# A two-layer decoder trunk on one core: longer planner estimates, all low parts on VectorE, other warming products

## The chip, the cores and the metric

The kernel runs on one core of one Trainium2 chip. The metric is the device time of one execution in microseconds (us), smaller being better. A core has a matrix engine (TensorE, PE in the rows; PEld is its weight load), VectorE (DVE), ScalarE (ACT), GpSimd (POOL) and SyncE (SP), which here issues the weight DMAs. Each engine works through its own instructions in the order in which the program holds them and waits on semaphores for the others.

## What is computed

256 tokens of width 1024 go through two layers in float32. Cut to what matters:

```python
for layer in range(2):
    y = h @ w_in[layer]                       # 3672 columns, split among three head groups
    out_a = gla_mixer(...)                    # gated linear attention, 4 heads, chunks of 64
    out_b = moba_mixer(...)                   # one causal block of 256: softmax attention, 4 heads
    out_c = dsa_mixer(...)                    # indexer scores, the best 64 keys of a query, softmax
    mix = concat(out_a, out_b, out_c) @ w_out[layer]
    h = layer_norm(2 ** 0.5 * h + mix)
    h = layer_norm(2 ** 0.5 * h + moe_ffn(h)) # 16 experts, best group, top 2, SiLU gate, d_ff 512
```

The DSA group keeps, for each query, the keys whose indexer score is among the 64 highest, and takes a softmax over them alone.

## The kernel before

**Stages.** A layer has a mixer stage (projections, the three mixers, the product with `w_out`) and an expert stage. The two token tiles of 128 rows are t = 0 and 1. All weights stream in over SP into 33 buffers of 512 KB and some small ones; a buffer's next load is issued when its last reader is done.

**Projections.** A weight slice of 128 x 512 is split into a high part (`whi`, ScalarE) and a low part (`wlo`, the difference) by `Pieces.fill`, four slices ahead of their use (three for `w_out`). Three products per token tile (high by high, high by low, low by high) make one projection (`pj`, `gq`, `gk`; `po` with `w_out`). The keys come in the order I (indexer), V, GV, M (MoBA's q and k), S (DSA's q and k), GK, GG. Low parts are made by VectorE, save each fifth from the 25th slice on, which GpSimd makes (`SHARE`, `FROM`, line 593): 13 a layer, and two more at the start of layer 1.

**Order.** The instructions of the mixer stage are not written in one order. `backbone` runs the projections, and tasks run beside it: `indexer` (scores, then eight rounds of MAX and MATCH_REPLACE on `acc` a tile, t = 1 first), `qk`, `decays`, `linear`, `gated`, and `attend`, which calls `softmax_pv` for S and M. Class `Order` keeps a clock per engine, advanced by `_Lane.cost`, an estimate in ns for each instruction. A task goes on as soon as what it waits for is due by PE's estimated clock. The rounds of the selection have one more condition, line 877: the estimated clock of VectorE may be at most 400 ns ahead of PE's. `attend` for S starts when the selections of both tiles are made (`done.add("sel")`).

**Softmax.** `softmax_pv` does t = 0 and then t = 1, each in full: four score products (`sc<-qkT`), on VectorE four row maxima with the mask (`s_sb,mx<-sc`), on ScalarE four exponentials, on VectorE the reciprocals and four scalings, on PE the transposes (`pT`), on ScalarE their copies; and at the end the products with the values (`pv`) and the split of the result into `mx` high and low.

**Output product.** `OUT_ORDER` is (4, 6, 2, 0): the two blocks of MoBA, then those of S, which wait for the split of S, then those of GLA (`mxG`).

**Routing.** After `po`, `close_mix` adds the residual, turns the result (`tr`), forms the router's logits (`lgT`, `lg`), and `score` applies a Sigmoid (`sc<-lg`). A one-element Sigmoid at the end of `gated` (tile `warm`) has ScalarE load that function's table ahead of time. `choose` picks experts and `xT` gathers tokens.

**Warming.** `warm(n, w)` issues 2n products of 128 x 128 whose result nobody reads: 14 at the start, 4 ahead of the routing's result in each layer, 8 between the layers.

Of the kernel before, what the change touches and what calls it, by code (L numbers as in the profile page):

```python
# [9 lines left out]
F32 = mybir.dt.float32  # L10
# [34 lines left out]
N_T4 = 9  # L45
N_SM = 10
N_WS = 4
SHARE = 5
FROM = 24
N_WO = 3  # L50
N_UNITS = ((1, 3), (2, 6))
N_WARM0 = 7
N_AHEAD = 5
LAG = 350.0
TRIG = 5487.999999999999
N_FILL = 2
N_LAST = 2
N_WARM = 2
N_LEAD = 7
N_WARM2 = 4  # L60
TWO = (1, 3, 5)
AGAIN = {(0, 'g', 5), (1, 'g', 2), (1, 'g', 0), (1, 'd', 1), (1, 'd', 6), (1, 'd', 4), (2, 'g', 3), (2, 'd', 6)}
FILL = (1, 2)
# [13 lines left out]
class Order:  # L77
# [24 lines left out]
    def note(self, lane, cost, ins, outs):  # L102
        start = self.clk[lane]
        for a in ins:
            t, who = self.ready.get(a.tensor.name, (0.0, lane))
            start = max(start, t + (self.NEAR[lane] if who == lane else self.FAR))
        end = start + cost
        self.clk[lane] = end
        for a in ins + outs:
            n = a.tensor.name  # L110
            if n in self.held:
                self.held[n] = max(self.held[n], end)
        for a in outs:
            self.ready[a.tensor.name] = max((end, lane), self.ready.get(a.tensor.name, (0.0, lane)))
# [74 lines left out]
class _Lane:  # L189
# [3 lines left out]
    def cost(self, name, out, ins, kw, scalars=0):  # L193
        def free(a):
            n = 1
            for s in a.shape[1:]:
                n *= s
            return n
        n = free(out)
        psum = any(i.space == bass.MemoryType.PSUM for i in ins)  # L200
        if self.lane == "PE":
            if name == "transpose":
                return 110.0
            f = 1.68 if ins[0].dtype == F32 else 0.42
            c = max(214.0 if ins[0].dtype == F32 else 100.0, f * n)
            if out.shape[0] <= 64 and ins[0].shape[0] <= 64 and n <= 128:
                return max(50.0, f * n / 2)
            return c / 2 + 20 if out.shape[0] <= 64 and ins[0].shape[0] > 64 else c
        if self.lane == "ACT":
            return 0.833 * n + (52 if psum else 94) + 93 * (scalars + ("accum_out" in kw))  # L210
        if self.lane == "POOL":
            if name == "memset":
                return 0.8 * n + 70
            return 165.0 * n + 300 if kw.get("op") == OP.pow else 2.2 * n + 50
        m = max([n] + [free(a) for a in ins])
        if name == "reciprocal":
            return 6.3 * n + 68
        if name in ("tensor_scalar", "tensor_copy") and not psum:
            return 0.54 * n + 65 + 61 * scalars
        return 1.04 * m + 65 + 61 * scalars  # L220

    def __getattr__(self, name):
        fn = getattr(self.e, name)
# [20 lines left out]
def trunk_kernel(ctx, tc, x, positions, w_in, gate_up, gate_bias, norm_gain, w_out, ln_mix_g, ln_mix_b,  # L244
# [8 lines left out]
    pe, act, dve, pool = od.pe, od.act, od.dve, od.pool  # L253
# [4 lines left out]
    def bank(name="ps"):  # L258
        b = pp.tile([P, 512], F32, name=name, tag="ps")
        od.take(b.tensor.name)  # L260
        return b

    def t2(name, shape=(P, 512), dt=F32):
        return wp.tile(list(shape), dt, name=name, tag="t2", bufs=N_T2)
# [80 lines left out]
    def more(n=1):  # L345
        for _ in range(n):
            while issued[0] < len(specs) and specs[issued[0]][0] in extra:
                issued[0] += 1
            if issued[0] >= len(specs):
                return  # L350
            key, (parts, nk, w) = specs[issued[0]]
            issued[0] += 1
            t = fp.tile([P, nk, w], F32, name="wf", tag="wf")
            for at, src in parts:
                nc.sync.dma_start(t[:, at[0], at[1]] if at else t.rearrange("p k n -> p (k n)"), src)
            feed[key] = t
# [66 lines left out]
    ident = cp.tile([P, P], F32, name="ident")  # L423
# [77 lines left out]
    def mm(o, a, b, start=True, stop=True):  # L501
        pe.matmul(o, a, b, start=start, stop=stop, skip_group_check=True)
# [59 lines left out]
    def warm(n, w):  # L562

        b_ = bank("warm")
        for i in range(2 * n):
            mm(b_[:, 0:P], w, ones)
        od.free(b_)

# [8 lines left out]
    class Pieces:  # L577
# [8 lines left out]
        def fill(self, eng=dve):  # L586
            while self.i < len(self.plan) and self.i < self.j + self.ahead:
                key, kk, c0, n = self.plan[self.i]
                src = feed[key][:, kk, c0:c0 + n]
                hi = t2("whi", (P, n), F32R)  # L590
                lo = t2("wlo", (P, n), F32R)
                act.activation(hi, src, AF.Copy)
                (pool if self.i % SHARE == SHARE - 1 and self.i >= FROM else eng).tensor_sub(lo, src, hi.bitcast(F32))
                units[key] = feed[key]
                self.made[self.i] = hi, lo
                self.left[key] -= 1
                if not self.left[key]:
                    feed.pop(key)
                    more()
                self.i += 1  # L600
# [72 lines left out]
    def weight_pieces(l):  # L673
        plan = []
        for key in ORDER:
            _, groups, cols = CHUNKS[key]
            for i, nk in enumerate(groups):
                plan += [((l, key, i), kk, cols[0] * j, n) for kk in range(nk) for j, n in enumerate(cols)]
        for k0 in OUT_ORDER:
            plan += [((l, "O", k0 + kk), 0, 512 * n, 512) for kk in range(2) for n in range(2)]  # L680
        return Pieces(plan, N_WS)
# [75 lines left out]

    units, begun = {}, set()
    warm(N_WARM0, ones)
    pieces = weight_pieces(0)  # L760
    hhi, hlo = halves(0)
# [4 lines left out]
    for l in range(DEPTH):  # L766
# [529 lines left out]
        def choose(t):  # L1296

            s, g = slice(t * E, t * E + E), slice(4 * t, 4 * t + 4)
            top1, top2 = (top[:, i:i + 1] for i in (2 * t, 2 * t + 1))
            x4 = sel[:, s].rearrange("p (g e) -> p g e", e=4)  # L1300
            xa, xj = (x4[:, :, :, None].to_broadcast([P, 4, 4, 4]), x4[:, :, None, :].to_broadcast([P, 4, 4, 4]))
            rank4 = rank[:, s].rearrange("p (g e) -> p g e", e=4)
            yield dve.tensor_add(sel[:, s], sc[:, s], rb)
            dve.tensor_add(sums[:, g, 0:2], x4[:, :, 0:2], x4[:, :, 2:4])
            dve.tensor_add(sums[:, g, 2:4], x4[:, :, 0::2], x4[:, :, 1::2])
            rev = bass.AP(tensor=sel.tensor, offset=sel.offset + t * E + 3, ap=[sel.ap[0], [4, 4], [-1, 2]])
            yield dve.tensor_add(sums[:, g, 4:6], x4[:, :, 0:2], rev)
            dve.tensor_reduce(gs[:, g], sums[:, g], AX.X, OP.max)
            yield dve.tensor_tensor(gt[:, g], xj, xa, op=OP.is_gt)
            dve.tensor_reduce(top1, gs[:, g], AX.X, OP.max)  # L1310
            yield dve.tensor_tensor(ge[:, g], xj, xa, op=OP.is_ge)
            dve.scalar_tensor_tensor(at[:, g], gs[:, g], top1, pref[:, 0:4], op0=OP.is_equal, op1=OP.mult)
            yield dve.copy_predicated(gt[:, g], below[:, None].to_broadcast([P, 4, 4, 4]), ge[:, g])
            dve.tensor_reduce(top2, at[:, g], AX.X, OP.max)
            yield dve.tensor_reduce(rank4, gt[:, g], AX.X, OP.add)
            yield dve.tensor_scalar(at[:, g], at[:, g], top2, None, op0=OP.is_ge)
            yield dve.scalar_tensor_tensor(hot[:, s].rearrange("p (g e) -> p g e", e=4), rank4, 1.5,
                                           at[:, g, None].to_broadcast([P, 4, 4]), op0=OP.is_lt, op1=OP.mult)
            if t == 0:
                mm(pc[:, 0:E], strict, hot[:, 0:E])  # L1320
            else:
                mm(pc[:, E:2 * E], strict, hot[:, E:2 * E])
            yield dve.tensor_scalar(pos[:, s], hot[:, s], -1000.0, 1000.0, op0=OP.mult, op1=OP.add)
            yield dve.tensor_add(pos[:, s], pos[:, s], pc[:, s])
# [165 lines left out]
        dve.tensor_scalar(mvs[1][:, 4:5], mvs[1][:, 0:1], mvs[1][:, 3:4], -1.0, op0=OP.mult, op1=OP.mult)  # L1490
        act.activation(h[1], h[1], AF.Identity, scale=mvs[1][:, 3:4], bias=mvs[1][:, 4:5])
        warm(N_WARM, ident)
        for _ in steps[0]:
            next(steps[1])
# [68 lines left out]
        for p in range(E // 2):  # L1563
# [54 lines left out]
            for i in range(8):  # L1618
                n, k = (i // 4, i % 4) if p >= FIN - 1 else (i % 2, i // 2)
# [39 lines left out]
        if last:  # L1659
            finish(z, sb, sts, *vecs[2:])  # L1660
            break
        warm(N_WARM2, ident)

        def close(t, z, st, hhi, hlo, nxt=l + 1, sb=sb, g2=vecs[2], b2=vecs[3]):
# [56 lines left out]
```

## Time and profile before

| what | value |
|---|---|
| median of 3 runs | 717.87 us (717.22 to 718.00) |
| profiled execution | 717.56 us, of which the span from the first to the last instruction 715.5 us |
| PE busy in the span | 687.1 us (96%) |
| VectorE, ScalarE, GpSimd busy | 443.9 us, 273.6 us, 75.0 us |
| mean granted TensorE clock | 0.993 of full speed |
| mixer stages, read off the timeline | about 6.8 to 148 us and 357 to 500 us |

A matmul's end in the trace is modelled, so PE busy time can hold short waits; the idle time before an instruction, in square brackets with what ended it, is what PE visibly waited. Float32 products show as two instructions each. Times in a timeline row are the start in the span and the length.

### The profile page before, as it was taken

What the parts mean: (1) busy time and instruction counts of PE and PEld (TensorE: products, weight loads), DVE (VectorE), ACT (ScalarE), POOL (GpSimd) and SP (SyncE); (2) the same over time, 40 slices, a digit from 0 to 9 for tenths busy, and PEclk for the clock granted to TensorE, in tenths of its full rate; (3) what the DMA queues carried; (4) which work ended last, traced back from release to release, by engine and by line L of the source; (5) the groups of instructions that cost most, each with busy time, mean ns of one, the idle gap of its engine ahead of it and who ended that gap; (6) DMA issues with size and microseconds to landing.
All of it is one profiled execution on the core that took longest, in us unless ns stands there. A gap on an engine that the chain in (4) does not pass through costs nothing. (4 is left out here: it accounts for less than half of the span.)

```text
span 715.5 us, 11300 instructions
## 1 busy us (share of the span) xinstructions
PE 687.1 (96%) x3885; PEld 399.2 (56%) x3885; DVE 443.9 (62%) x1091; ACT 273.6 (38%) x579; POOL 75.0 (10%) x102
## 2 busy tenths in 40 slices
PE   9999999999999989999899999999999999899993
PEld 8887878843533533533487879787435334343330
DVE  6778887652445454767487787867243556259646
ACT  5578675431212201212276676564223022022121
POOL 2021022200000001200121111121000000021002
PEclk9999999999999999999999999999999999999997
DMA  9799937979999999999999844479899999999971
GB/s 306 272 388 407 408 120 250 325 293 408 409 403 408 407 407 408 408 410 407 334 391 401 313 154 146 132 251 338 323 408 408 403 407 409 407 407 409 409 288 59
DMA packets 83533, 244.05 MB, mean 341 GB/s; under 512 B 10180, under 2 KB 14344, under 8 KB 83464
## 3 DMA queue, kind: packets, MB, share of 16 engines
q1 hardware_dynamic: 82792, 242.91, 89.0%
q8 instruction: 34, 0.56, 0.3%
q10 hardware_dynamic: 416, 0.26, 0.1%
q14 instruction: 35, 0.29, 0.1%
q0 software_dynamic: 256, 0.03, 0.0%
HBM read 242.13 MB, written 1.05 MB: 340 GB/s over the span
## 5 line engine op out<-in xcount | busy, mean ns | idle before, releaser
L239 PE MATMUL gu<-wf,xT 128*64 128x512 f32 x912 | 226.0, 594 | 3.6 <-PEq L1437 3.6
L239 DVE SCALAR_TENSOR_TENSOR yt<-y,ws,yt 32x512 fp32r<-32x512 f32 (+1 forms) x116 | 86.7, 748 | 94.9 <-ACT yt L239 93.4
L239 PEld LDWEIGHTS gu<-wf,xT 128*64 128x64 f32 x912 | 71.8, 137 | 131.7 <-issue 123.3
L239 DVE TENSOR_TENSOR wlo<-wf,whi 128x512 fp32r<-128x512 f32 (+3 forms) x148 | 89.6, 640 | 39.5 <-ACT whi L239 28.5
L239 PE MATMUL y<-wf,actT 128*64 128x512 f32 x432 | 110.5, 595 | 1.8 <-ACT actT L239 1.8
L239 ACT ACTIVATE whi<-wf 128x512 fp32r<-128x512 f32 (+3 forms) x176 | 86.1, 553 | 9.8 <-PE po L239 3.6
L239 PE MATMUL pj<-whi,hhi 128*128 128x512 f32 (+2 forms) x224 | 77.4, 356 | 0.4 <-ACT whi L239 0.4
L239 ACT ACTIVATE yt<-y,ws 128x512 fp32r<-128x512 f32 x60 | 36.8, 687 | 104.5 <-PE y L239 94.9
L239 PE MATMUL pj<-whi,hlo 128*128 128x512 f32 (+2 forms) x224 | 75.4, 347 | 0.0
L239 PEld LDWEIGHTS y<-wf,actT 128*64 128x64 f32 x432 | 34.0, 137 | 54.1 <-issue 42.0
L239 DVE TENSOR_TENSOR act<-act,gu 128x512 f32<-128x512 f32 x16 | 11.0, 688 | 83.7 <-PE gu L239 77.1
L239 PE MATMUL pj<-wlo,hhi 128*128 128x512 f32 (+2 forms) x224 | 60.5, 356 | 0.4 <-DVE wlo L239 0.4
L239 POOL TENSOR_TENSOR wlo<-wf,whi 128x512 fp32r<-128x512 f32 (+3 forms) x28 | 32.4, 1158 | 220.1 <-ACT whi L239 183.6
L239 PE MATMUL gu<-wx,xT 128*64 128x512 f32 x112 | 52.7, 596 | 0.0
L239 PEld LDWEIGHTS pj<-whi,hhi 128*128 128x128 f32 x224 | 42.1, 188 | 7.3 <-issue 1.7
L239 PEld LDWEIGHTS pj<-whi,hlo 128*128 128x128 f32 x224 | 42.1, 188 | 4.7
L239 ACT ACTIVATE actT<-aT 128x512 f32<-128x512 f32 x16 | 9.5, 594 | 85.4 <-PE aT L239 85.4
L239 PEld LDWEIGHTS pj<-wlo,hhi 128*128 128x128 f32 x224 | 37.5, 188 | 6.6 <-issue 1.2
L239 ACT ACTIVATE xT<-xT,cols 128x256 f32<-128x256 f32 x32 | 17.4, 564 | 57.2 <-PE xT L239 57.2
L239 ACT ACTIVATE act<-gu 128x512 f32<-128x512 f32 x16 | 9.6, 597 | 75.9 <-PE gu L239 75.9
L239 PE MATMUL y<-wx,actT 128*64 128x512 f32 x80 | 33.4, 595 | 0.0
L239 DVE TENSOR_TENSOR z<-z,sc 128x512 f32<-128x512 f32 x48 | 29.7, 680 | 0.4 <-PE sc L239 0.4
(268 smaller groups left out, 948.1 us busy)
## 6 DMA issues: line engine op xcount, KB each, us to landing
wf<-in_w_expert_gate_dram SPq DMA_DIRECT2D x114, 512.0 KB, 10.2
wf<-in_w_expert_up_dram SPq DMA_DIRECT2D x114, 512.0 KB, 10.1
wf<-in_w_expert_down_dram SPq DMA_DIRECT2D x108, 512.0 KB, 10.0
wf<-in_w_in_dram SPq DMA_DIRECT2D x32, 512.0 KB, 9.8
wx<-in_w_expert_down_dram SPq DMA_DIRECT2D x36, 256.0 KB, 5.9
wf<-in_w_out_dram SPq DMA_DIRECT2D x16, 512.0 KB, 11.1
wx<-in_w_expert_up_dram SPq DMA_DIRECT2D x24, 256.0 KB, 6.9
wx<-in_w_expert_gate_dram SPq DMA_DIRECT2D x10, 512.0 KB, 10.1
```

The lines of the kernel that those rows point to most:

```text
L239: return fn(*a, **kw)
```

## The change

The planner's estimates grow: ScalarE's fixed part from 52 to 150 ns for reads of PSUM and from 94 to 110 ns otherwise, VectorE's from 65 to 155 ns for reads of PSUM. Every low part goes to VectorE, except the two at the start of layer 1. `warm(n)` issues n products instead of 2n; with the new counts this is 11 at the start (before: 14), 4 and 8 as before, and 2 new ones in each layer behind the count of the first tile's chosen experts.

```diff
-SHARE = 5
-FROM = 24
-N_WARM0 = 7
+N_WARM0 = 11
+N_KEEP = 2
-N_WARM = 2
+N_WARM = 4
-N_WARM2 = 4
+N_WARM2 = 8
...
         if self.lane == "ACT":
-            return 0.833 * n + (52 if psum else 94) + 93 * (scalars + ("accum_out" in kw))
+            return 0.833 * n + (150 if psum else 110) + 93 * (scalars + ("accum_out" in kw))
...
-        return 1.04 * m + 65 + 61 * scalars
+        return 1.04 * m + (155 if psum else 65) + 61 * scalars
...
-        for i in range(2 * n):
+        for i in range(n):
             mm(b_[:, 0:P], w, ones)
...
-                (pool if self.i % SHARE == SHARE - 1 and self.i >= FROM else eng).tensor_sub(lo, src, hi.bitcast(F32))
+                eng.tensor_sub(lo, src, hi.bitcast(F32))
...
             if t == 0:
                 mm(pc[:, 0:E], strict, hot[:, 0:E])
+                warm(N_KEEP, ident)
```

The new estimates give another order in the mixer stage. On PE, at the end of layer 0's mixer stage (line 239 of the kernel before and 238 of the one after are the same recording helper; `sc<-qkT` here are the scores of S, t = 1), it stood before:

```order
L239 MATMUL sc<-qkT 128x256 x4
L239 MATMUL kv<-W,kd 64x128 x4
L239 MATMUL pj<-wlo,hhi 128x512 x2
L239 MATMUL pj<-whi,hhi 128x512
L239 MATMUL pj<-whi,hlo 128x512
L239 MATMUL kv<-W,kd 64x128 x4
```

Behind the scores stand projections and the sums of GLA's state, which wait for nothing in the softmax. The transposes and the products with the values of the same softmax come 16 rows later:

```order
L239 MATMUL pT<-ident,s_sb 128x128 x8
L239 MATMUL pv<-pT,v 64x128 x12
L239 MATMUL pj<-whi,hhi 128x512
L239 MATMUL pj<-whi,hlo 128x512
L239 MATMUL pj<-whi,hhi 128x512
```

Behind these too stand projections. The same place now, where `sc<-qkT 128x128` are the scores of S for t = 0:

```order
L238 MATMUL po<-wlo,mx 128x512
L238 MATMUL sc<-qkT 128x128 x4
L238 MATMUL tr<-ident,og 128x128 x8
L238 MATMUL pT<-ident,s_sb 128x128 x4
L238 MATMUL sc<-qkT 128x256 x4
L238 MATMUL pT<-ident,s_sb 128x128 x8
L238 MATMUL pv<-pT,v 64x128 x12
L238 MATMUL po<-whi,mx 128x512 x2
```

The whole softmax of S, both tiles, has moved from between the last projections to between the output products of MoBA and those of S; layer 1 has the same rows there.

On VectorE, what stands ahead of the row maxima of S, t = 0, in layer 0 now (`acc` is the selection of t = 0; before, its last round stood ahead of MoBA's maxima for t = 1, and the maxima of S, t = 0, followed two low parts later):

```order
L238 TENSOR_TENSOR og<-o,ms 128x512
L238 TENSOR_TENSOR wlo<-wf,whi 128x512
L238 MAX m_962<-acc 128x8
L238 MATCH_REPLACE acc<-m_962,acc 128x128
L238 TENSOR_SCALAR acc<-acc 128x128
L238 TENSOR_TENSOR acc<-acc,mc 128x128
L238 TENSOR_REDUCE ms<-sq 128x4
L238 TENSOR_SCALAR ms<-ms 128x4
L238 TENSOR_TENSOR wlo<-wf,whi 128x512
L238 ISA s_sb,mx<-sc,acc 128x128
```

Of the eight rounds of the selection for t = 0, the last ones have moved behind the start of `linear`, and the maxima of S with them.

On ScalarE, layer 0, before (`sg` is the SiLU gate, `warm` the one-element Sigmoid):

```order
L239 ACT_TABLE_LOAD
L239 ACTIVATE sg<-pj 128x512 x2
L239 ACTIVATE whi<-wf 128x512 x4
L239 ACTIVATE mxG<-tr,cols 128x4x128
L239 ACTIVATE whi<-wf 128x512
L239 ACTIVATE mxG<-tr,cols 128x4x128
L239 ACT_TABLE_LOAD
L239 ACTIVATE warm<-mhalf 128x1
```

There one load serves the gate and one the Sigmoid. Now it reads, from behind the SiLU gate on:

```order
L238 ACT_TABLE_LOAD
L238 ACTIVATE s_sb,mx<-s_sb,mx 128x128 x4
L238 ACTIVATE mxG<-tr,cols 128x4x128 x2
L238 ACT_TABLE_LOAD
L238 ACTIVATE warm<-mhalf 128x1
L238 ACTIVATE pT<-pT 128x512
L238 ACT_TABLE_LOAD
L238 ACTIVATE s_sb,mx<-s_sb,mx 128x256 x4
```

The exponentials of both tiles have moved behind the gate and the second tile's behind the Sigmoid, each with a load of their table ahead of them. A third load has come further on, in the routing, where before the Sigmoid stood right behind `zT`:

```order
L238 ACTIVATE zT<-tr 128x4x128
L238 ACT_TABLE_LOAD
L238 ACTIVATE sc<-lg 128x16
L238 ACTIVATE lsb<-lgT 128x128
L238 ACTIVATE h<-h,mv 128x512
```

The Sigmoid's table has to be loaded again there, since the exponentials of the second tile have come after `warm`: three table loads more in each layer than before.

## Rows read from the trace of the kernel before

**Rows 1.** Busy time by stretch: stretch, length, PE (instructions), PEld, DVE, ACT, POOL, clock, DMA.

```profile
6.80:140.00 133.20, 131.99 (x868) 109.37 (x867) 105.57 (x300) 87.26 (x203) 18.64 (x19) 1.00 0.86 313
356.70:490.00 133.30, 130.57 (x860) 108.49 (x859) 103.40 (x274) 87.93 (x205) 26.05 (x22) 1.00 0.72 258
60.00:80.00 20.00, 19.25 (x105) 15.44 (x104) 19.22 (x59) 14.19 (x32) 2.58 (x3) 1.00 1.03 409
160.00:340.00 180.00, 177.93 (x876) 70.92 (x873) 94.89 (x183) 36.10 (x63) 8.63 (x13) 1.00 1.03 407
```

**Rows 2.** Timeline, a softmax of tile 0: start, length, engine, operation, idle before.

```profile
75.55 0.28 DVE L239 CUSTOM_DVE_ANT_0 s_sb<-sc,mc 128x128 f32<-128x128 f32 x1
...
76.71 0.40 ACT L239 ACTIVATE s_sb<-s_sb,mx 128x128 f32<-128x128 f32 x1 [2.08 <-DVE mx L239]
```

**Rows 3.** Timeline, GLA's result in layer 0, on three engines.

```profile
121.25 1.28 DVE L239 TENSOR_TENSOR og<-og,sg 128x512 f32<-128x512 f32 x2
...
124.32 0.75 DVE L239 SCALAR_TENSOR_TENSOR mxG<-tr,cols,mxG 128x512 fp32r<-128x512 f32 x1
...
124.78 0.60 PE L239 MATMUL tr<-ident,og 128*128 128x128 f32 x4
...
125.41 0.69 ACT L239 ACTIVATE mxG<-tr,cols 128x512 fp32r<-128x512 f32 x1 [0.61 <-PE tr L239]
...
126.12 1.28 ACT L239 ACT_TABLE_LOAD   x1
```

**Rows 4.** Timeline, four scalings of 128 columns, beside GpSimd and alone.

```profile
79.98 1.30 POOL L239 TENSOR_TENSOR wlo<-wf,whi 128x512 fp32r<-128x512 f32 x1 [9.72 <-ACT whi L239]
80.02 1.93 DVE L239 TENSOR_SCALAR s_sb<-s_sb,ri 128x128 f32<-128x128 f32 x4
...
97.76 0.87 DVE L239 TENSOR_SCALAR s_sb<-s_sb,ri 128x128 f32<-128x128 f32 x4
```

**Rows 5.** Timeline, softmax of S, tile 1, layer 0, from scores to split.

```profile
101.75 1.13 PE L239 MATMUL sc<-qkT 64*128 64x256 f32 x8
...
105.10 0.51 ACT L239 ACTIVATE s_sb<-s_sb,mx 128x256 f32<-128x256 f32 x1
...
108.34 0.17 DVE L239 RECIPROCAL ri<-mx 128x4 f32<-128x4 f32 x1
...
108.55 1.15 DVE L239 TENSOR_SCALAR s_sb<-s_sb,ri 128x256 f32<-128x256 f32 x4
...
110.92 1.03 PE L239 MATMUL pT<-ident,s_sb 128*128 128x128 f32 x8
...
111.56 1.08 ACT L239 ACTIVATE pT<-pT 128x512 f32<-128x512 f32 x2 [1.42 <-PE pT L239]
...
111.89 1.58 PE L239 MATMUL pv<-pT,v 128*64 128x128 f32 x24
...
113.50 0.60 ACT L239 ACTIVATE mx<-pv 128x512 fp32r<-128x512 f32 x1 [0.35 <-PE pv L239]
...
114.14 0.69 DVE L239 TENSOR_TENSOR mx<-pv,mx 128x512 fp32r<-128x512 f32 x1 [0.25 <-ACT mx L239]
```

**Rows 6.** Timeline, the start: TensorE's products on ones and ScalarE's first work.

```profile
1.05 5.88 PE L239 MATMUL warm<-ones 128*128 128x128 f32 x28 [1.05 <-POOL ones L363]
...
5.50 0.78 ACT L239 ACTIVATE whi<-wf 128x292 fp32r<-128x292 f32 x2 [2.94 <-DMA wf<-in_w_in_dram]
```

**Rows 7.** Busy time by stretch, the last microseconds, columns as in rows 1.

```profile
702.00:706.00 4.00, 1.49 (x6) 0.59 (x4) 2.51 (x6) 0.69 (x1) 0.58 (x1) 1.00 0.00 0
706.00:708.00 2.00, 0.00 (x0) 0.00 (x0) 1.97 (x6) 1.45 (x2) 1.20 (x3) 0.51 0.00 0
```

**Rows 8.** Timeline, routing of layer 0.

```profile
143.12 0.60 ACT L239 ACTIVATE zT<-tr 128x512 f32<-128x512 f32 x1 [0.37 <-PE tr L239]
143.61 0.21 ACT L239 ACTIVATE sc<-lg 128x16 f32<-128x16 f32 x1
...
147.24 1.18 PE L239 MATMUL xT<-G,h 128*128 128x128 f32 x8 [1.08 <-DVE top L239]
```

## Prediction, made before the changed kernel ran

> **What bounds the kernel now.** I read three views in turn. First the busy time by stretch: in both mixer stages PE works 131.99 us of 133.20 and 130.57 of 133.30, in the experts' stage 177.93 of 180 [rows 1]. So TensorE alone sets the time nearly everywhere: 1.21 and 2.73 us of idle time in the mixer stages are all that a better order there could win back. VectorE has 105.57 and 103.40 us of work in the same stretches, ScalarE 87.26 and 87.93; both have room on the whole, though from 60 to 80 us VectorE is busy 19.22 of 20 [rows 1]. Second, the timeline of a softmax, to see how long its steps take when they are followed one behind another [rows 2, 5], and of GLA's result [rows 3]. Third, the order of the instructions, which is the change itself. The trace of before can show what a step costs; the order of the changed kernel shows which steps no longer have anything beside them.
>
> **The order, which carries the sum.** Before, the scores of S (t = 1) went out at 101.75 and the transposes of the same softmax at 110.92, nine microseconds later [rows 5], with projections between them; PE never stood still for it. Now all of S, tiles 0 and 1, stands behind the output products of MoBA, and between its scores, transposes and `pv` there is no projection left. PE works strictly in order, so the 66 further `po` products wait behind it. What PE then waits for is the chain, which I count from the first score product of t = 0.
>
> To the scores of t = 1: scores half as wide as those of t = 1, 0.57 (half of 1.13 [rows 5]) and 0.08 to VectorE's read; row maxima until the first exponential 1.16 (75.55 to 76.71 [rows 2]). VectorE doesn't go to the scalings then: `og` and the gate's products of GLA stand ahead of them, 0.64 for `og` and 0.64 for the first of two gate products (each half of 1.28 [rows 3]); from the transposes to ScalarE's read of them 0.63 (124.78 to 125.41), two `mxG` on ScalarE 2 x 0.69, the last on VectorE 0.75 [rows 3]. The four exponentials at 0.40 [rows 2] fit beside this. Then reciprocal 0.17 [rows 5], four scalings 0.87 [rows 4], the last transpose and the start of the scores about 0.2. Sum 7.1.
>
> From there to the output products: scores to the first exponential 3.35 (101.75 to 105.10), four exponentials 4 x 0.51, reciprocal 0.17, scalings 1.15, the last transposes with their copy about 1.0 (a copy is half of 1.08), from the copies' end (111.56 + 1.08) to `mx` on ScalarE 0.86 (113.50), from there to the end of the low half 1.33 (114.14 + 0.69 less 113.50), all [rows 5]; less 0.23, since the first product needs only the high half. Sum 9.7.
>
> Together 16.8 us. PE's own work in it has only been moved: scores 0.57 and 1.13, transposes 2 x 0.60 [rows 3], 0.52 (half of 1.03) and 1.03, `pv` 1.58 [rows 5], 6.0 by the rows' lengths. These include the tail of the last product of each row, some 0.1 apiece, so I take 5.5. New idle time: 16.8 - 5.5 = 11.3 us a layer, **22.6 us** for two. Bounds: 9 a layer if VectorE does `og` while ScalarE is still at work and the steps overlap more (the two tiles' copies and `pv` by halves), 14 if `og` of the second tile isn't ready and the rounds of the selection ahead of the maxima are late.
>
> **The clock.** [...] At the program's start 28 records on ones take 5.88 us, 0.21 each [rows 6], where four transposes of the same size take 0.60 with their tail [rows 3]; so for some 5.9 us PE ran at about half rate, though steadily busy, which costs half of that, 2.9. Upper bound 5.1 a layer, lower bound 0. I take 4, since rows 7 are near to this case: **8.0 us** for two.
>
> **Table loads.** A load takes 1.28 us on ScalarE [rows 3]. The first of the three new ones (for the exponentials of t = 0) stands behind the SiLU gate and runs while PE is still at MoBA's products: 0. The second (t = 1) stands behind the copy of the first tile's transposes and ends about 7.1 + 1.0 + 1.28 = 9.4 after the start of the chain, while the maxima come at 7.1 + 3.35 = 10.5: 0, with 1.1 to spare. The third stands in the routing between `zT`, which ends at 143.72, and the first tile's Sigmoid at 143.61 [rows 8]: it would then begin at about 145.00, 1.4 later. Its tile's choice is what PE waits for already (1.08 ahead of `xT` [rows 8]), so the full 1.4 shows, **2.8 us** for two. The load at 126.12 begins 0.02 us after `mxG` ended (125.41 + 0.69 [rows 3]), so the row shows no pause ahead of it, and none is in the sum.
>
> **Low parts.** GpSimd loses 13 subtractions a layer, VectorE gets them. One of 128 x 512 takes 0.69 on VectorE [rows 5], so 13 x 0.69 = 9.0 us go on top of 105.57 and 103.40 of 133 [rows 1]. Against that, four scalings took 1.93 beside GpSimd's subtraction and 0.87 alone [rows 4]: at most 13 x 1.06 = 13.8 us a layer come off. Both lie beside PE's work as long as slices are made four ahead, and PE's idle time there is 1.21 and 2.73 us. I take **-1.0** for both layers: the gain can't be over 3.9, the whole of that idle time, and 3 us of loss would need the dense stretches to run over.
>
> **Warming.** Six fewer records at the start are 6 x 0.21 = 1.26 us [rows 6]. The first weights are there at 5.50 [rows 6], before the products on ones end, so the projections begin earlier; but they too start at the slow rate, so I take **-0.8** (0 to -1.26). The two new products in each routing lie in the 1.08 us in which PE waits [rows 8]: 0, and 0.4 a layer if not. The new order at the start of layer 1 (all transposes of `z` ahead of the projections) moves work within VectorE's closing: 0, within 1.
>
> **Sum.** 22.6 + 8.0 + 2.8 - 1.0 - 0.8 = 31.6 on the profiled 717.56, 749.2. That execution lies 0.3 below the median of the runs, 717.87: **749.5**.
>
> **Rivals.** (A) The order does what it says, but TensorE's clock holds through the chain, since PE has a burst of products every few microseconds: the 8.0 falls away, 741.5. For it: at 702 to 706 the clock was still 1.00 with PE busy 1.49 [rows 7]. Against it: the next stretch shows 0.51. (B) VectorE becomes the bound in the projections. It has 19.22 of 20 us in its densest stretch [rows 1], and if of its 9.0 us a layer 40%, 3.75, falls into such stretches and PE waits for low parts, the time is 749.5 + 7.5 = 757. Against it: GpSimd's relief is as large. (C) The other side, not slower: the experts' stage gives the delay back. Weights arrive there at 407 GB/s with a DMA share of 1.03 [rows 1], the engines' limit; if it were the stream that sets that stage, every microsecond PE loses in the mixer stage is one in which weights come in early, and the time would stay at 717.9, or some 2 us lower with the start and the relief. It decides only if PE waits for weights 16 us a layer in the experts' stage now; it is idle 2.07 of 180 [rows 1]. (D) A table load costs a pause of its own length besides: 1.28 more in the routing, and in the chain 1.28 less the 1.1 to spare, 0.2, in each layer; 3.0 in all, 752.5. Against it stands the 0.02 us ahead of the load at 126.12 [rows 3]. [...]
>
> **How the numbers follow.** Forecast with the clock falling for part of the chain 0.71; A 0.17; B 0.07; C 0.03; D 0.02. The likeliest gives 749.5. Range: low end, clock held and a chain of 9 instead of 11.3 a layer with some more relief, 741.5 - 3.5 = 738; high end, a chain of 14 would give 755, and B's part or the full 5.1 of the clock with it 759. Within 0.2% (1.4 us, about what a measurement of this kernel can tell from no change) or faster stands only C: faster 0.01, same 0.02, slower 0.97.
>
> **What would show it.** In the profile of the changed kernel PE's row by slices should have a dent near 125 to 145 us and again some 375 us later, with PE busy about 5.5 of 17 us, waiting on VectorE's scalings, then ScalarE's `pT` and VectorE's `mx`; the granted clock in these stretches decides between the forecast and A. The Sigmoid in the routing should have a load ahead of it and `xT` a wait of some 2.5 us. GpSimd should have two low parts left. If `po` waits on `wlo` or projections on VectorE, B is right; if the stage of the experts is shorter by what the mixers lost, C; if ScalarE stands idle beside a load for as long as the load takes, D. The forecast is wrong in its base if PE finds the results of the softmax ready when it comes to the transposes.

## The result, and the profile after

The changed kernel takes 748.8 us (median of 4 runs, 744.84 to 750.67) against 717.93 for the kernel before on the same chip: 1.042 times as long, 95% interval 1.0388 to 1.045. The forecast was 749.5 with a range of 738 to 759. The profiled execution took 748.0 us, its span is 746.3, 30.8 more than before.

Where the time went, by the starts of the first projection (`pj`), the last product before the routing (`po`), the first gather (`xT`) and the first expert product (`gu`) in the two timelines:

| stretch | before, us | after, us | difference |
|---|---|---|---|
| start to first projection | 6.76 | 5.91 | -0.85 |
| layer 0, projections to last `po` | 134.21 | 147.75 | +13.54 |
| layer 0, last `po` to `xT` | 6.27 | 7.70 | +1.43 |
| layer 0, `xT` to first expert | 4.06 | 6.44 | +2.38 |
| experts and closing | 205.39 | 207.00 | +1.61 |
| layer 1, projections to last `po` | 136.45 | 145.82 | +9.37 |
| layer 1, last `po` to `xT` | 6.27 | 7.86 | +1.59 |
| layer 1, `xT` to first expert | 4.06 | 5.56 | +1.50 |
| layer 1, experts to the end | 212.01 | 212.21 | +0.20 |

The nine differences add up to the 30.8.

First the busy time by stretch of the kernel after (columns as in [rows 1]), through layer 0's chain and then through its routing:

```profile
112.00:116.00 4.00, 4.00 (x30) 3.06 (x29) 3.83 (x11) 2.75 (x4) 0.04 (x1) 1.00 0.89 330
116.00:120.00 4.00, 1.59 (x15) 1.02 (x13) 3.26 (x13) 1.67 (x9) 1.34 (x1) 1.00 0.42 134
120.00:124.00 4.00, 1.97 (x12) 1.26 (x10) 2.47 (x8) 2.77 (x4) 0.00 (x0) 0.79 0.00 0
124.00:128.00 4.00, 1.97 (x8) 1.07 (x8) 1.63 (x9) 2.18 (x3) 0.00 (x0) 0.50 0.00 0
128.00:132.00 4.00, 1.48 (x7) 1.51 (x8) 1.32 (x5) 2.07 (x9) 0.00 (x0) 0.50 0.00 0
132.00:136.00 4.00, 3.31 (x28) 2.58 (x26) 0.06 (x1) 1.59 (x4) 0.00 (x0) 0.51 0.00 0
136.00:140.00 4.00, 3.78 (x16) 2.89 (x17) 4.00 (x7) 3.02 (x6) 0.00 (x0) 1.00 0.24 70
...
156.00:158.00 2.00, 0.69 (x16) 0.16 (x8) 0.21 (x2) 1.97 (x4) 0.55 (x1) 1.00 1.06 388
158.00:160.00 2.00, 1.38 (x10) 1.21 (x11) 1.93 (x16) 0.92 (x3) 0.00 (x0) 0.96 1.06 408
160.00:162.00 2.00, 1.87 (x8) 1.60 (x8) 1.92 (x17) 1.31 (x2) 0.00 (x0) 0.50 0.65 258
162.00:164.00 2.00, 2.00 (x11) 1.94 (x11) 0.89 (x5) 0.00 (x0) 0.00 (x0) 0.50 0.03 10
164.00:166.00 2.00, 2.00 (x12) 2.00 (x11) 0.00 (x0) 0.00 (x0) 0.00 (x0) 0.50 0.00 0
166.00:170.00 4.00, 4.00 (x25) 2.45 (x25) 2.85 (x10) 3.35 (x5) 0.00 (x0) 0.92 0.02 4
```

From 116 to 136 us no engine is busy throughout, and PE is busy less than half of the time to 132: the mark of a chain. The granted clock (third column from the right) falls to 0.50 inside it and is back at 1.00 at 136. It falls to 0.50 once more at 160, in the routing, where PE is busy again; the prediction hadn't looked for that.

The chain itself, as a timeline of layer 0 (start, length, engine, operation, idle before and what ended it), beside [rows 5]:

```profile
119.56 1.26 PE L238 MATMUL tr<-ident,og 128*128 128x128 f32 x8 [2.41 <-DVE og L238]
...
120.25 1.29 ACT L238 ACTIVATE mxG<-tr,cols 128x512 fp32r<-128x512 f32 x2 [0.26 <-PE tr L238]
120.97 1.41 DVE L238 SCALAR_TENSOR_TENSOR mxG<-tr,cols,mxG 128x512 fp32r<-128x512 f32 x2 [0.87 <-ACT mxG L238]
...
122.50 0.87 DVE L238 TENSOR_SCALAR s_sb<-s_sb,ri 128x128 f32<-128x128 f32 x4
122.84 1.12 PE L238 MATMUL pT<-ident,s_sb 128*128 128x128 f32 x4 [2.03 <-DVE s_sb L238]
...
123.89 2.08 PE L238 MATMUL sc<-qkT 64*128 64x256 f32 x8
124.05 0.60 ACT L238 ACTIVATE pT<-pT 128x512 f32<-128x512 f32 x1 [1.00 <-PE pT L238]
124.67 1.28 ACT L238 ACT_TABLE_LOAD   x1
...
127.70 0.51 ACT L238 ACTIVATE s_sb<-s_sb,mx 128x256 f32<-128x256 f32 x1 [1.75 <-DVE mx L238]
...
130.52 1.94 PE L238 MATMUL pT<-ident,s_sb 128*128 128x128 f32 x8 [4.55 <-DVE s_sb L238]
...
132.39 2.88 PE L238 MATMUL pv<-pT,v 128*64 128x128 f32 x24
...
135.96 0.50 PE L238 MATMUL po<-whi,mx 128*128 128x512 f32 x1 [0.69 <-ACT mx L238]
```

The steps come in the order in which the prediction counted them. The eight score products take 2.08 us here and 1.13 in [rows 5], `pv` 2.88 against 1.58, at a granted clock of 0.50 and 0.51 here and of 1.00 there (the kernel before from 100 to 120 us). The first score of t = 0 starts at 116.43, so the chain is 19.53 us long, and 19.10 in layer 1 (483.81 to 502.91).

And the routing, beside [rows 8]:

```profile
155.82 0.60 ACT L238 ACTIVATE zT<-tr 128x512 f32<-128x512 f32 x1 [0.37 <-PE tr L238]
...
156.44 1.28 ACT L238 ACT_TABLE_LOAD   x1
...
157.73 0.21 ACT L238 ACTIVATE sc<-lg 128x16 f32<-128x16 f32 x1
...
158.16 0.40 PE L238 MATMUL lg<-fold,lsb 128*128 128x16 f32 x2 [1.27 <-ACT lsb L238]
```

The load stands between `zT` and the Sigmoid, and PE waits 1.27 us for `lsb`, which is queued on ScalarE behind the load.

### The profile page after: what moved, and what is told of

Its sections match the earlier page's. It is cut to its first block, busy times and chain, and to the rows that moved or that the text cites. A ratio compares the mean times of both kernels' runs of the same rounds, so it can differ in the third digit from the quotient of the medians.

```text
span 746.3 us, 11275 instructions
## 1 busy us (share of the span) xinstructions
PE 700.8 (94%) x3887; PEld 410.4 (55%) x3887; DVE 444.9 (60%) x1117; ACT 282.9 (38%) x585; POOL 44.3 (6%) x76
## 3 DMA queue, kind: packets, MB, share of 16 engines
HBM read 242.13 MB, written 1.05 MB: 326 GB/s over the span
## 5 line engine op out<-in xcount | busy, mean ns | idle before, releaser
L238 DVE TENSOR_TENSOR wlo<-wf,whi 128x512 fp32r<-128x512 f32 (+3 forms) x174 | 99.4, 616 | 50.5 <-ACT whi L238 43.1
## 6 DMA issues: line engine op xcount, KB each, us to landing
wf<-in_w_expert_gate_dram SPq DMA_DIRECT2D x114, 512.0 KB, 10.1
wf<-in_w_expert_up_dram SPq DMA_DIRECT2D x114, 512.0 KB, 10.1
```

The source lines that it names most:

```text
L238: return fn(*a, **kw)
```

## The experiments

The theory was that the loss is the softmax of S without cover (cover is other work that TensorE has in its queue while the softmax goes through the other engines), the clock that falls there, and the load in the routing. Rivals were VectorE's added work, and the chain's own length without any part of the clock. Before is always the kernel before on the same chip (717.9 in the first four, 718.0 in the next four, 717.68 in the last). The kernel after stands at 748.8 throughout, measured beside 717.93.

### Is it the order? Four orders from one kernel

The four runs keep the low parts on VectorE and the new products on ones, and change numbers of the planner.

```diff
-                    yield lambda: od.clk["DVE"] <= od.clk["PE"] + 400
+                    yield lambda: od.clk["DVE"] <= od.clk["PE"] + 4000
```

> The kernel after with one number changed: VectorE's estimated clock may be 4000 ns instead of 400 ahead of TensorE's for a round of the selection. The planner then puts the whole softmax of S back among the projections (scores of t = 1 ahead of 26 or more projection products before their transposes) and has no extra table load. All longer estimates, all low parts on VectorE and the new products on ones stay. Theory (the loss is the exposed softmax of S, its clock and the table load in the routing): all of that goes and only the gains at the start (0.85 us) and in the projections (about 3 us) stay, 712 to 717 us. Rival (VectorE's extra low parts or the new order elsewhere cost time by themselves): 725 us or more.

Measured: 733.88 us (732.54 to 735.08). The theory's 712 to 717 is missed; by its number the rival came out, 725 or more, the new order elsewhere costing time by itself. The chain is gone all the same: from first to last `po` layer 0 takes 24.71 us (149.87 less 125.16), against 23.46 before and 44.01 in the kernel after; the routing takes 6.27 and 4.15 again. But layer 0 needs 119.25 us from the first projection to the first `po`, before 110.75. Layer 1 shows the same, 117.91 against 111.75. What PE waits for from 30 to 120 us and from 368 to 487 us there, as total, times and longest, and the timeline of one such wait:

```profile
PE pj L238 <- DVE wlo L238: 6.5, 4, 2.6
PE pj L238 <- DVE wlo L238: 8.4, 6, 2.2
```

```profile
37.45 0.43 DVE L238 MAX8 m<-acc 128x8 f32<-128x256 f32 x1
...
37.91 0.28 PE L238 MATMUL pj<-wlo,hhi 128*128 128x256 f32 x1
...
39.42 0.43 DVE L238 MAX8 m<-acc 128x8 f32<-128x256 f32 x1
...
39.96 0.41 DVE L238 MATCH_REPLACE8 acc<-m,acc 128x256 f32<-128x256 f32 x1
40.28 1.45 DVE L238 TENSOR_TENSOR wlo<-wf,whi 128x272 fp32r<-128x272 f32 x4
40.77 0.63 PE L238 MATMUL pj<-wlo,hhi 128*128 128x272 f32 x3 [2.58 <-DVE wlo L238]
```

Three rounds of the selection run from 37.45 to 40.28 ahead of four low parts that PE needs. So the condition on the rounds is a price on both sides: at 400 with the longer estimates the selection of t = 0 comes too late for S, at 4000 the rounds come in bursts and the low parts too late for the projections. These waits are 14.9 of the 16 us. The granted clock from 30 to 60 us is 0.92 here and 1.00 before, so a part of the rest is the clock again.

The other three runs set estimates back to those of before. In the next diff the first line is ScalarE's estimate and the second VectorE's; one run changes both, the other two one each.

```diff
-            return 0.833 * n + (150 if psum else 110) + 93 * (scalars + ("accum_out" in kw))
+            return 0.833 * n + (52 if psum else 94) + 93 * (scalars + ("accum_out" in kw))
...
-        return 1.04 * m + (155 if psum else 65) + 61 * scalars
+        return 1.04 * m + 65 + 61 * scalars
```

Both lines:

> The kernel after with the estimates of before; all low parts on VectorE and the products on ones as after. The planner still moves the selection later, since it counts VectorE's added subtractions: the scores of S, t = 1, stand behind 12 output products and their transposes 12 products and the products of GLA's second tile later, so about 3.8 us of the 5.9 us from scores to transposes are covered; no load in the routing. Theory (the price is what of the chain has no cover): 2 to 5 us a layer lost, 3 to 4 us gained as in the kernel after, 718 to 725 us. Rival (the longer estimates alone move the softmax): at or below 717 us. Rival (VectorE's load costs the time): about 745 us.

Measured: 722.92 us (722.5 to 723.19), as the theory has it. PE waits 2.1 us for the scalings ahead of the transposes of S, t = 1, and 1.4 ahead of GLA's, in layer 0. The estimates are thus not alone in moving the softmax: the planner counts the low parts on VectorE too.

The second line alone (ScalarE's estimate stays long):

> The kernel after with VectorE's estimate of before and ScalarE's longer one. By the order the scores of S, t = 1, stand 4 projection products and 24 output products and one tile of GLA ahead of their transposes, some 7.4 us, against 5.9 us needed; no extra table load. Theory (uncovered chain): near nothing is lost, 713 to 719 us. Rival (VectorE's load): 740 us or more.

Measured: 717.68 us (717.48 to 718.36), ratio 0.9995 (0.9986 to 1.0005): the same as before, as the theory has it. Beside the run ahead of it ScalarE's longer estimate takes 5.2 us off: in layer 0 the scores of S, t = 1, stand 10.23 us ahead of their transposes instead of 7.22 (108.02 to 118.25, and 114.22 to 121.44), and PE doesn't wait for the scalings.

The first line alone (VectorE's estimate stays long):

> The kernel after with ScalarE's estimate of before and VectorE's longer one. By the order the scores of S, t = 0, stand 12 output products earlier than in the kernel after, everything behind them as there, with the load in the routing. Theory (uncovered chain): the first part of the chain is covered by about 2.8 us, the rest is as in the kernel after, 741 to 748 us. Rival (both estimates are needed for the loss): below 730 us.

Measured: 748.62 us (746.97 to 749.81), as slow as the kernel after. The theory's size was off (741 to 748). From the first `po` to the output products of S the run gains 1.6 us in layer 0 and 1.1 in layer 1, less than the 2.8 of cover: the scores start at 113.58, but VectorE takes up their maxima at 115.76 only, behind GLA's sums (in the kernel after 0.74 us lie between the two). And the gain is lost again. In layer 0 the clock isn't back when the output products of S start (0.50 from 132 to 136 us and 0.68 to 140, in the kernel after 0.51 and 1.00); a pair takes 1.05 us where it takes 0.62 in the kernel after, and from first to last `po` both kernels need 44.0 us:

```profile
134.47 1.52 PE L238 MATMUL po<-whi,mx 128*128 128x512 f32 x2 [0.69 <-ACT mx L238]
...
136.21 1.05 PE L238 MATMUL po<-whi,mx 128*128 128x512 f32 x2
```

Layer 1 loses 1.9 us in its projections. So VectorE's longer estimate, with the low parts on VectorE, is what takes the cover away; ScalarE's adds nothing measurable to it. Whether it would do so with low parts on GpSimd wasn't run.

### What does the clock cost, and what the load?

```diff
-            act.activation(sm("warm", 1), mhalf[:, 0:1], AF.Sigmoid)
...
+        if v0 == 256:
+            nc.scalar.activation(sm("warm", 1), mhalf[:, 0:1], AF.Sigmoid)
         st.add("mix%d" % v0)
```

> The kernel after with the one-element Sigmoid issued behind the split of S's result instead of behind GLA's; the planner still counts it at its old place, so the order of everything else is as in the kernel after. The Sigmoid's table then stays loaded for the routing, and the load ahead of the exponentials of t = 1 goes too. Theory (the load delays the routing by 1.4 us a layer and its idle time lets TensorE's clock fall, 2.4 and 1.5 us more): 3.0 + 3.9 = 6.9 us less than the kernel after on the same chip, about 742 us. Rival (the clock falls in the routing anyway, as an echo of the chain): 3.0 us less.

Measured: 743.9 us (743.33 to 745.18), 4.9 less than the kernel after, between the theory's 6.9 and the rival's 3.0. By stretch the theory's 6.9 is there: the last `po` to `xT` takes 6.28 in both layers, `xT` to the first expert 4.10, and the clock in the routing is 1.00. But the chain is 20.19 and 20.05 us long in this profile, 0.7 and 1.0 more than after. In layer 0 the clock fell earlier: it is 0.87 from 116 to 120 us, where the kernel after has 1.00. In layer 1 it is 0.52, 0.63, 0.80, 0.50 and 0.50 in the five stretches of 4 us from 484 to 504, and isn't back until about 504.6 (0.92 from 504 to 508), 3.7 us into the output products of S, which costs 1.4 us more. Without the load the clock stayed at 1.00 in the routing of both layers, although it had fallen to 0.50 in the chain.

```diff
+    def keep(n, b_):
+        for _ in range(n):
+            nc.tensor.matmul(b_[:, 0:P], ones, ones, start=True, stop=True, skip_group_check=True)
...
                 b_ = bank("tr")
                 b3 = b_.rearrange("p (a n) -> p a n", a=4)
+                keep(9 * (t == 0), b_)
...
                 b_ = bank("pT")
+                if v0 == 256 and h0 == 0:
+                    keep(19 if t else 7, b_)
```

> The kernel after with products on ones, whose result nobody reads, where TensorE waits in the chain: 9 ahead of the transposes of GLA's first tile, 7 ahead of those of S, t = 0, and 19 ahead of those of S, t = 1, in each layer; all else in the same order. Theory (the clock falls because TensorE idles in the chain): the clock stays at its upper level there and the chain goes from 19.5 and 19.1 to about 17 us, 4 to 5 us less than the kernel after, 744 us; the fall in the routing stays. Rival (the chain is long for its own steps and the clock costs little): no difference within 1 us. If the products run over the waits they add up to 1 us a layer.

Measured: 740.53 us (738.07 to 740.78), 8.3 less than the kernel after, where 4 to 5 were expected. The chain is 16.31 and 16.32 us long. They give 6.0 of it, and in the profiled execution (738.07, the fastest of the four) the fall in the routing, which was expected to stay, is nearly gone too: the clock is 0.85 and 0.72 from 152 to 160 us in layer 0, and 1.00 throughout in layer 1.

```diff
                 pls.append(bank("lg"))
+                keep(5 * t, pls[t])
                 mm(pls[t][:, 0:E], lsb[t], fold)
```

> As the run before, and 5 products on ones ahead of the second tile's logits in the routing, where TensorE waits 1.27 us. Theory (the fall in the routing comes from the idle time that the table load makes): the clock stays up there too and another 3.9 us go, about 740 us; the 1.4 us of the load in each layer stay. Rival (it falls for another reason): as the run before.

Measured: 738.73 us (737.84 to 740.43), 10.1 less than the kernel after; `xT` to the first expert takes 4.10 in both layers, but it does so in the run before too (4.07 and 4.10), so the products in the routing weren't needed for it. Busy time by stretch of the two chains, first in this run and then in the kernel after:

```profile
116.30:132.60 16.30, 14.91 (x132) 12.78 (x131) 8.28 (x35) 10.14 (x26) 0.90 (x1) 1.00 0.10 34
479.70:496.10 16.40, 15.01 (x132) 12.84 (x131) 8.37 (x35) 10.18 (x26) 0.94 (x1) 1.00 0.10 33
```

```profile
116.40:136.00 19.60, 9.92 (x62) 7.38 (x61) 8.35 (x35) 10.27 (x26) 0.94 (x1) 0.65 0.08 27
483.80:502.90 19.10, 9.48 (x61) 6.95 (x60) 8.37 (x35) 10.30 (x26) 0.92 (x1) 0.64 0.09 29
```

With 70 more records in each, the stretch is 3 us shorter: VectorE and ScalarE have the same work in it, and the clock is 1.00 instead of 0.65. That is the price of the clock in the chain, 3.2 and 2.8 us, and products that do nothing saved it where TensorE waits in the chain.

### The low parts and the start alone

```diff
-                (pool if self.i % SHARE == SHARE - 1 and self.i >= FROM else eng).tensor_sub(lo, src, hi.bitcast(F32))
+                if self.i % SHARE == SHARE - 1 and self.i >= FROM:
+                    pool.e = nc.vector
+                    pool.tensor_sub(lo, src, hi.bitcast(F32))
+                    pool.e = nc.gpsimd
+                else:
+                    eng.tensor_sub(lo, src, hi.bitcast(F32))
```

> The kernel before with its 26 low parts issued on VectorE instead of GpSimd; the planner still counts them on GpSimd, so that the order of all instructions is that of before. This is the low parts' change alone. Theory (relief of VectorE's scalings beside GpSimd is worth more than the added 9 us a layer, all beside TensorE's work): 714 to 717.5 us. Rival (VectorE becomes late in its dense stretches): 719 to 725 us.

Measured: 719.31 us (717.63 to 719.53), ratio 1.0006 (0.9987 to 1.0025): no difference that can be told from noise. The median lies at the edge of the rival's 719 to 725, but neither a gain nor a loss is measured. In the page's first part and among its costliest groups (count, busy, mean ns):

```profile
PE 687.3 (96%) x3885; PEld 399.3 (56%) x3885; DVE 444.3 (62%) x1117; ACT 274.1 (38%) x579; POOL 45.1 (6%) x76
...
L239 DVE TENSOR_TENSOR wlo<-wf,whi 128x512 fp32r<-128x512 f32 (+3 forms) x174 | 97.6, 599 | 43.4 <-ACT whi L239 41.7
```

VectorE has 26 subtractions more than before and is busy 444.3 us instead of 443.9. Two of its groups by shape, first in the kernel before and then in this run:

```profile
L239 DVE TENSOR_TENSOR wlo<-wf,whi 128x512 fp32r<-128x512 f32 x94 | 67.2, 740 | 30.8 <-ACT whi L239 19.9 <-issue 7.5 <-PE po L239 2.4
L239 DVE TENSOR_SCALAR s_sb<-s_sb,ri 128x128 f32<-128x128 f32 x16 | 4.6, 347 | 0.1
```

```profile
L239 DVE TENSOR_TENSOR wlo<-wf,whi 128x512 fp32r<-128x512 f32 x112 | 73.8, 687 | 33.2 <-ACT whi L239 31.5 <-PE po L239 1.3
L239 DVE TENSOR_SCALAR s_sb<-s_sb,ri 128x128 f32<-128x128 f32 x16 | 3.5, 283 | 0.1
```

```diff
-N_WARM0 = 7
+N_WARM0 = 5.5
...
-        for i in range(2 * n):
+        for i in range(int(2 * n)):
```

> The kernel before with 11 instead of 14 products on ones at the start, all else and the whole order as in the kernel before. This is the start's change alone. Theory (the first weights are there before those products end): 0.85 us less than the kernel before, about 717.1 us. Rival (the projections at the start run at the low clock for longer and give it back): no difference within 0.3 us.

Measured: 717.36 us, ratio 1.0003 (0.9986 to 1.0021): the same. The interval reaches from 1.0 us less to 1.5 more, so the time alone excludes neither side. In the trace the projections start at 5.54 instead of 6.76, but the first `po` comes only 0.51 earlier (117.00 against 117.51), so more than half is given back. The column of the granted clock shows no low clock there: it is 1.00 over the first 12 us, in the kernel before and in the one after. What is slow is the single record: 0.21 us each on ones at the start ([rows 6]), and 8 in 1.14 us, 0.14 each, in the routing of the kernel before (`warm` at 144.83).

### Is there a better condition?

The same line as in the first experiment, with 2000; with 4000 for the rounds of t = 0 only; and with 2000 for them only:

```diff
-                    yield lambda: od.clk["DVE"] <= od.clk["PE"] + 400
+                    yield lambda: od.clk["DVE"] <= od.clk["PE"] + 2000
```

> The kernel after with 2000 instead of 400 in the condition of the selection's rounds. By the order all of S stands among the projections, with no extra table load, and rounds come in shorter bursts than with 4000. Theory (in the run with 4000 the time went into low parts queued behind rounds on VectorE, 2 to 2.7 us a time, four to five times a layer; four slices of lead cover a burst of 2000): 714 to 721 us. Rival (with the longer estimates any looser condition costs as much): 728 us or more.

Measured: 720.11 us (718.83 to 720.83), inside the theory's 714 to 721, with waits for low parts of 0.6 us in all in layer 0's projections and 2.9 in layer 1's.

```diff
+                    yield lambda: od.clk["DVE"] <= od.clk["PE"] + (400 if t else 4000)
```

> The kernel after with 4000 only for the rounds of t = 0, 400 for t = 1 as in the kernel after. The order then has S among the projections. A burst of eight rounds of t = 0, 0.57 us each, is 4.6 us, near the lead of four slices. Theory (bursts of rounds delay low parts): no or one wait of about 2 us a layer, 715 to 723 us. Rival (the placing of S among the projections costs by itself): 728 us or more.

Measured: 721.79 us (720.17 to 722.43), inside the theory's 715 to 723: PE waits for low parts twice in each layer's projections, 1.5 us in layer 0 and 2.1 in layer 1.

```diff
+                    yield lambda: od.clk["DVE"] <= od.clk["PE"] + (400 if t else 2000)
```

> The kernel after with 2000 for the rounds of t = 0 and 400 for t = 1. By the order the scores of S, t = 1, stand 16 projection products and 12 output products ahead of their transposes, about 7.5 us with GLA's, against 5.9 us needed. Theory (uncovered chain, no bursts): 713 to 718 us, at or below the kernel before. Rival: as with 4000 for t = 0.

Measured: 718.05 us (716.65 to 718.49), ratio 0.9997 (0.9985 to 1.0008), at the upper end of the theory's 713 to 718: the whole loss is mended by one number, with all of the change's estimates, low parts and products in place, but nothing is won over the kernel before. Layer 0's scores of S, t = 1, and their transposes are here (projections and output products stand between them, and PE doesn't wait):

```profile
106.73 1.13 PE L238 MATMUL sc<-qkT 64*128 64x256 f32 x8
...
116.92 1.04 PE L238 MATMUL pT<-ident,s_sb 128*128 128x128 f32 x8
```

No run beat the kernel before measurably.

## Why the prediction was right

**The chain, right.** Counted 16.8 us from rows of before, 16.3 at the full clock (16.30 and 16.31 in the run with both fillings), 7.1 against 7.26 to the scores of t = 1 and 9.7 against 9.04 from there. With the forecast's 5.5 us of PE's own work the idle time is 10.8 a layer, where 11.3 was forecast: 21.6 us instead of 22.6. The traces bear the 5.5 out: from the first projection to the last `po` of layer 0 PE is busy 133.4 us before and 127.7 after outside the chain, 5.7 less. The mended order, with everything else of the change, takes the time back to 718.05, so the order is shown to be the cause, not only argued.

**The clock, right in sum, wrong in place.** Forecast 8.0, all of it for the chain. No run shows this term or its upper bound of 5.1 a layer; the runs show 3.2 and 2.8 in the chain, and `po` behind the chain at 1.00 at once (the stretch from 136), so a slow stretch like the start's 2.9 is nothing here. It isn't always: with VectorE's longer estimate alone `po` of layer 0 lost 1.6 us to it, with the late Sigmoid `po` of layer 1 lost 1.4. Beside the chain comes a second fall, to 0.50, in the routing, 2.4 and 1.5 us, which the prediction hadn't: it took the load's wait as idle time only. Together 9.9, and the run with both fillings is 10.1 us faster than the kernel after (8.7 between the two profiled executions). That 8.0 came near 9.9 is thus partly luck. Rival A (the clock holds), 741.5, is what the fillings make true: 738.73.

**The loads, right.** 1.43 and 1.59 us between last `po` and `xT`, forecast 1.4 each. The load ahead of the exponentials of t = 1 ends at 125.95, the maxima are ready for them at 127.70, so it is covered, by 1.75 us. Rival D is out: `zT` ends at 156.42, the load begins at 156.44, the Sigmoid at 157.73, so 1.31 us lie between them, the load's 1.28 and 0.03 more.

**Low parts, no effect; projections, mis-sized.** The -1.0 was given to the low parts' relief. Alone they change nothing. Two effects cancel on VectorE: its 128 x 512 subtractions average 740 ns before and 687 without GpSimd's low parts beside them, its scalings of 128 columns fall from 347 to 283 ns on the mean, and 26 subtractions are added. For four scalings [rows 4] agree, 1.93 us beside a subtraction on GpSimd and 0.87 alone; the sum over the kernel is those 443.9 and 444.3 us. Why VectorE is slower beside GpSimd isn't shown. The kernel after still gains 2.9 us outside of the chain, the routing and the start (-0.5 and +1.6, -4.2 and +0.2 in the table with the chain's 14.0 and 13.6 taken off). It agrees with the idle time up to the first `po` of each layer, 1.21 and 2.73 us before, 0.66 and none after, 3.3 less in all (stretch, length, PE; before, then after):

```profile
6.76:117.51 110.75, 109.54 (x762) 90.59 (x761) 90.46 (x277) 74.97 (x183) 13.93 (x16) 1.00 0.87 319
356.69:468.44 111.75, 109.02 (x750) 90.89 (x749) 88.81 (x253) 75.12 (x184) 19.65 (x18) 1.00 0.69 253
```

```profile
5.91:109.65 103.74, 103.08 (x693) 86.21 (x692) 81.93 (x245) 69.16 (x164) 1.88 (x5) 1.00 0.91 338
374.80:477.03 102.23, 102.23 (x691) 85.69 (x689) 81.26 (x220) 68.76 (x162) 6.57 (x6) 1.00 0.75 271
```

That the new order does this was not tried apart, and stays open. The +1.61 ahead of layer 1 is the closing, 6.03 us before and 7.66 after, where the transposes of `z` now all stand; the prediction had put it at nothing, within 1.

**The start.** -0.85 in the trace, -0.8 forecast; alone it isn't measurable. The two new products in each routing cost nothing, as forecast: with them and without the load, `xT` comes 6.27 us after the last `po` (ScalarE's longer estimate alone), as before.

Sum: 21.6 + 9.9 + 3.0 - 2.9 - 0.85 = 30.75, the span grew by 30.8. (The 2.9 is what the table leaves over, so the sum can't miss by much; what bears it out are the 3.3 us of idle time.) The forecast's 31.6 is near for a partly lucky reason: the chain was 1.0 too long, the clock 1.9 too small, the projections 1.9 too small a gain. B fails: `po` and projections don't wait for low parts in the kernel after. C fails: the experts' stage gives nothing back, 199.3 us from the first `gu` to the closing in both kernels.

Some figures of the prediction don't follow from its terms, and none of them decides anything: a chain of 9 us takes 4.6 off A's 741.5, which is 736.9 and not 738; 40% of 9.0 is 3.6 and not 3.75, so B stands at 756.7; the additions named for the high end give some 757 or 762 and not 759; and 72 output products stand behind the chain, 66 of them ahead of the first transposes.

## What to carry to other kernels

A softmax that goes through three engines cost its full length here, 19.53 and 19.10 us, where nothing stood beside it on the engine that bounds; its price can be summed step by step from a trace in which it is still hidden. In a planner that orders by estimated clocks, estimates, conditions and assignments of work act through the order: compare orders, not constants, and look for work without cover at the end of a stage; a condition that balances two consumers of one engine has to be set again when an estimate changes. Where the chain had no cover, products that do nothing kept the matrix engine's granted clock at 1.00 (0.65 and 0.64 without them), and paid 8 to 10 us.

## What the runs showed of the hardware

- In the routing the clock fell in layers where both the chain had brought it down (it was back some 20 to 24 us earlier) and the load stood in the routing (PE waits 1.27 us there in both layers of the kernel after): to 0.50 in 4 of 4 layers of two kernels (the kernel after and the one with VectorE's longer estimate). Without the load (2 layers) and with the chain kept busy and the routing filled (2 layers) it stayed at 1.00; with the chain kept busy and the routing not filled it fell for a short time in one of 2 (0.85 and 0.72 from 152 to 160 us). Which of the two conditions decides isn't settled by so few layers.
- The four runs of the kernel after spread over 5.8 us, and their times follow the granted clock: 744.84 us at 0.972, 748.0 at 0.966, 749.59 at 0.965, 750.67 at 0.963.
- In layer 0 of the kernel after PE's clock came back behind `pv` (0.51 from 132 to 136 us, with PE busy 3.31 of 4, then 1.00). In one layer of two of the run with VectorE's longer estimate, and of the one with the late Sigmoid, it came back only under `po` behind the chain, at some 138.6 and 504.6 us (worked out from 0.68 in the stretch from 136 to 140 and 0.92 from 504 to 508).
